# Two-layer hybrid trunk on one core: VectorE and ScalarE in the program's own order, and a weight tile's residual emitted with its load

## The chip, the cores and the metric

The kernel runs on one core of one Trainium2 chip. The metric is the device time of one execution in microseconds (us). A core has a tensor engine (TensorE, "PE" in the profile, its weight loads "PEld"), VectorE ("DVE"), ScalarE ("ACT"), GpSimd ("POOL") and SyncE ("SP"), which issues the transfers. The engines run side by side, each through its own instructions in the order in which they were emitted to it, and wait for one another by semaphores.

## The reference

256 tokens of width 2048 go through two layers. Each layer has a token mixer (layer 0: forgetting attention with 16 heads of 128; layer 1: grouped-query attention with 32 heads of 64 in a window of 128, with sinks and partly rotated positions) and a gated ConvFFN of inner width 5632. Cut to what matters:

```python
c_act = silu(c)
for i in range(2):
    mod = c_act @ ada_w[i] + ada_b[i]            # 2048 -> 6 x 2048
    sh1, sc1, g1, sh2, sc2, g2 = split(mod, 6)
    h = x * (1 + sc1) + sh1
    y = fox_attention(h) if i == 0 else swa_attention(h)
    x = layer_norm(alpha * x + (1 + g1) * y)
    h = x * (1 + sc2) + sh2
    y = conv_ffn(h)     # u = conv3(h @ w_up) + b; (silu(u[:5632]) * u[5632:]) @ w_down
    x = layer_norm(alpha * x + (1 + g2) * y)
# fox_attention: q, k, v, f = split(h @ w_in); C = cumsum(log_sigmoid(f + b))
#   softmax(q k^T / sqrt(128) + C_t - C_s, causal) @ v, then @ w_o
```

All data are float32.

## The kernel before, in words

**Products in three parts.** Each float32 operand of a large product is split into a high part and a residual. For a weight tile the high part `wh` is a cast on ScalarE (L254), and the residual `wl` = `w` − `wh` a subtraction on VectorE (L265). TensorE (L75, `mm`) then adds three products: high with high, high with residual, residual with high. The same split is made of activations by `split`: cast on ScalarE (L84), subtraction on VectorE (L85).

**Weight tiles.** `stream` loads weights through SyncE in tiles of 128x1024 values (two of the kernel's rows of tiles of 512 columns) into a pool of six 1 MB buffers, which the adaLN weights (`wa`) share. `wh` and `wl` have four buffers each. For each tile `stream` emits the load and the cast at once and appends a function `go` to the list `work`. `settle(2)` runs the oldest entries of `work` until no more than two tiles are outstanding. Before it runs one, `rest(f, *work)` emits the residuals of that tile and of the next ones, up to three tiles. `go` then runs the deferred work that is due (`run_post`), the products of the tile (`use`), one entry of `feeds`, and `tick`.

**What `tick` adds.** It hands out side work at a rate per weight tile: an adaLN column (L364, on VectorE, 128x2048), gate rows, and pieces of attention heads. A head of layer 0 is: scores `S`; two passes on VectorE that mask and find the maximum (L609, 128x128 and 128x256, with a readout `nm`); two exponentials with sums on ScalarE (L613); the reciprocal of the sums on VectorE (L621); two scalings on ScalarE (L623); transposes on TensorE (`T`, L640) and their copy (`pT`, L642); the product with the values, split into `oT`. Layer 1's heads come in pairs in a similar way (L609, L613, L961 to L972), with queries turned and split (`qT`, `qL`).

**Evacuations.** `evac_qk` adds the two halves of a projection on VectorE (`sum`, L756), and splits the sum: `qh` on ScalarE (L759 or L84), `ql` on VectorE (L760 or L85). The FFN's evacuation has a scaled copy `u` on ScalarE (L1006), two steps of the convolution on VectorE (L1007, L1009), the SiLU on ScalarE (L1025) for the gate half, the product (L1030) and the split into `gT` (L84, L85) for the other half.

**Between sub-layers.** `residual` (L537 multiply, L539 add, L544 to L549 statistics) evacuates the output projection by blocks of 512 columns, for token halves t = 0 and t = 1; then rows are normalised, modulated and split (`hH`). At the end of the program the last LayerNorm is written as a loop over t and four blocks, each with two operations on VectorE (L1095, L1096) and its transfer out.

**What sets the order.** The kernel is written for a framework that takes the program's order as a start and then lets a scheduler of its own order the instructions of each engine by when it expects them to be ready. Single instructions are held in place by `pin` (L78 to L81). Of the residuals (`residual_`) only those are held that are emitted while `behind[0] > 0`. The line that could take whole engines out of the scheduler's hands stands at the top, with an empty list, so that it does nothing.

Of the kernel before, what the change touches and what calls it, by code (L numbers as in the profile page):

```python
# [40 lines left out]
@with_exitstack  # L41
def hybrid_trunk(ctx: ExitStack, tc: tile.TileContext, a: dict, out: bass.AP):
    nc = tc.nc
    if []:
        ctx.enter_context(tc.manual_schedule(engines={getattr(mybir.EngineType, e) for e in []}))
    f32 = lambda t: t.bitcast(F32)

    cst = ctx.enter_context(tc.tile_pool(name="cst", bufs=1))
# [7 lines left out]
    def wtile(name="w"):  # L56
        return wp.tile([P, UK, WB], F32, tag="w", name=name)
# [19 lines left out]
    def pin(ins, on=True):  # L77

        if on:
            tc.keep_in_program_order(ins)  # L80
# [103 lines left out]
    feeds, post, work = [], [], []  # L184
# [11 lines left out]
    def settle(left=0):  # L196
        while work and (ahead[0] > left or not left):
            f = work.pop(0)
            rest(f, *work)
            f()  # L200

    def rest(*items):

        n = 0
        for f in items:
            if f in lone:
                n = max(n, 2)
            if f in residuals:
                residuals[f]()
                n += 1  # L210
            elif f in weights:
                n += 1
            if n > 2 - (items[0] not in weights):
                return
# [7 lines left out]
    def run_post():  # L222
        for g in list(post):
            if next(g, post) is post:
                post.remove(g)
# [7 lines left out]
    def stream(wsrc, row0, col, ks, use, spare={}):  # L233

        ks, pend = list(ks), {}
        for kc in ks[::2]:
            g = row0 + kc
            src = wsrc[g // UK, col // WB]
            if kc in pend:
                w = pend[kc]  # L240
            elif g % UK == 0 and kc + 2 in ks:
                W = wtile()
                pin(nc.sync.dma_start(W, src), False)
                w, pend[kc + 2] = W[:, :2], W[:, 2:]
            else:
                if halves:
                    w = halves.pop()
                else:
                    W = wtile()
                    w = W[:, :2]  # L250
                    halves.append(W[:, 2:])
                pin(nc.sync.dma_start(w, src[:, g % UK:g % UK + 2]), False)
            h, l = spare.get(kc) or (hl.tile([P, 2, WB], F32R, tag=n, name=n) for n in ("wh", "wl"))
            pin(nc.scalar.copy(h, w), False)  # L254

            def go(kc=kc, h=h, l=l):
                ahead[0] -= 1
                run_post()
                use(kc, h, l)
                if feeds:  # L260
                    feeds.pop(0)()
                tick()

            def residual_(w=w, h=h, l=l, go=go):
                pin(nc.vector.tensor_tensor(l, w, f32(h), op=ALU.subtract), behind[0] > 0)  # L265
                behind[0] -= 1
                del residuals[go]

            ahead[0] += 1
            weights.add(go)  # L270
            residuals[go] = residual_
            work.append(go)
            settle(2)

    def x_mm(ps, kc, h, l, stat, last, first=0, ts=range(NT), js=range(2)):
# [37 lines left out]
    def x_stationary(wsrc, col, k0, nk, stat, end=0):  # L313

        ps = x_banks()
        use = x_mm_end(ps, stat, nk, end) if end else lambda kc, h, l: x_mm(ps, kc, h, l, stat, nk - 1)
        stream(wsrc, k0, col, list(range(nk)), use, spares(nk) if end == 8 else {})
        return ps

    def w_stationary(wsrc, col):  # L320

        ps = w_banks()
        stream(wsrc, 0, col, list(range(KC)), lambda kc, h, l: w_mm(ps, kc, h, l))
        return ps
# [24 lines left out]
    def tick():  # L349
        ada_tick()  # L350
        if not feeds:
            side_step()
            step()
# [300 lines left out]
    def out_proj(oT, full, w_o, l):  # L654
        def stat(kc, t):
            while kc not in full:
                step()
            return oT[kc][0][:, t * P:(t + 1) * P], oT[kc][1][:, t * P:(t + 1) * P]

        ps = {d: x_banks() for d in range(2)}  # L660

        def part(d, ks):
            use = x_mm_end(ps[d], stat, KC, 2) if d == D // WB - 1 else                 lambda kc, h, l_: x_mm(ps[d], kc, h, l_, stat, KC - 1)
            stream(w_o, 0, d * WB, ks, use)

        for i, ks in enumerate((range(0, 8), range(8, 12))):
            then(lambda i=i: ada.update(rate=(0.72, 0.43)[l]))
            for d in range(2):
                part(d, list(ks))
        then(lambda: (ada_need(l, 2), ada.update(rate=(0.72, 0.65)[l])))  # L670
        for d in range(D // WB):
            if d < 2:
                part(d, list(range(12, KC)))
            else:
                ps[d] = x_banks()
                part(d, list(range(KC)))
            then(lambda d=d: defer(residual(ps[d], d, gates[l, 2], True)), d == D // WB - 1)
        then(lambda: (flush(), ada.update(gate_free=True)), True)
# [462 lines left out]
```

## Time and profile before

| what | value |
|---|---|
| median of 3 runs | 2195.59 us (2195.2 to 2195.61) |
| the profiled execution | 2194.81 us |
| its span | 2193.0 us |
| mean granted TensorE clock | 0.993 |
| busy TensorE / weight loads | 2138.1 us (97%) / 1948.5 us (89%) |
| busy VectorE / ScalarE | 1764.0 us (80%) / 1161.5 us (53%) |
| weight tiles split | 724 (`wh` 761.4 us on ScalarE, `wl` 879.4 us on VectorE) |
| adaLN columns | 192 (449.4 us on VectorE) |
| read from HBM | 594.18 MB, 272 GB/s over the span |

The span is the time from the first to the last instruction of the profiled execution; its own time is 1.8 us longer. Busy times are summed per engine over the whole span, so they average over stages which differ: the stages of layer 0's heads, the two FFNs, layer 1's heads and the transitions. In a group's line stand the line of the kernel, the engine, the operation, what is written and read (partitions x elements), the count, then busy us and mean ns of one, then the idle time of the engine just before and what ended it.

### The profile page before, as it was taken

What the parts mean: (1) busy time and instruction counts of PE and PEld (TensorE: products, weight loads), DVE (VectorE), ACT (ScalarE), POOL (GpSimd) and SP (SyncE); (2) the same over time, 40 slices, a digit from 0 to 9 for tenths busy, and PEclk for the clock granted to TensorE, in tenths of its full rate; (3) what the DMA queues carried; (4) which work ended last, traced back from release to release, by engine and by line L of the source; (5) the groups of instructions that cost most, each with busy time, mean ns of one, the idle gap of its engine ahead of it and who ended that gap; (6) DMA issues with size and microseconds to landing.
All of it is one profiled execution on the core that took longest, in us unless ns stands there. A gap on an engine that the chain in (4) does not pass through costs nothing.

```text
span 2193.0 us, 36167 instructions
## 1 busy us (share of the span) xinstructions
PE 2138.1 (97%) x14694; PEld 1948.5 (89%) x14694; DVE 1764.0 (80%) x2412; ACT 1161.5 (53%) x1771; POOL 11.5 (1%) x34
## 2 busy tenths in 40 slices
PE   6999999899999999999999999999999999999997
PEld 6999887689999888999987877789999988999986
DVE  7988899989989888898998876679787655666765
ACT  4546566355575433555554577555556533555541
POOL 1000000000000000000000000000000000000000
PEclk9999999999999999999999999999999999999999
DMA  9998999958878898887998653458776555555552
GB/s 385 421 373 307 359 340 338 346 205 343 325 281 324 325 364 341 321 316 284 329 349 308 238 189 130 154 175 305 272 268 248 192 194 193 195 197 196 193 196 98
DMA packets 89657, 598.63 MB, mean 273 GB/s; under 512 B 10017, under 2 KB 12353, under 8 KB 21137
## 3 DMA queue, kind: packets, MB, share of 16 engines
q1 hardware_dynamic: 89312, 595.87, 73.5%
q8 instruction: 115, 1.88, 0.3%
q0 software_dynamic: 176, 0.44, 0.1%
q14 instruction: 54, 0.43, 0.1%
HBM read 594.18 MB, written 2.10 MB: 272 GB/s over the span
## 4 chain that ended last, share of the span: by engine, by line
PE 85%; DVE 9%; ACT 3%; issue 2%; DMA 2%; SPq 0%; POOL 0%; DVEq 0%; ACTq 0%; POOLq 0%
PE ws L75 46%; PE xs L75 35%; DVE wa L364 3%; DVE wl L265 3%; DMA w<-in_fox_w_in_dram 2%; ACT wh L254 1%; PE o L75 1%; PE T L640 1%; PE S L75 1%; PE sm L446 0%; DVE x L581 0%; ACT pr L613 0%; DVE x L582 0%; DVE x L539 0%; DVE stats L544 0%
## 5 line engine op out<-in xcount | busy, mean ns | idle before, releaser
L254 ACT CAST wh<-w 128x1024 fp32r<-128x1024 f32 x724 | 761.4, 1053 | 804.4 <-PE xs L75 372.1
L265 DVE TENSOR_TENSOR wl<-w,wh 128x1024 fp32r<-128x1024 f32 x724 | 879.4, 1221 | 349.3 <-ACT wh L254 346.0
L75 PE MATMUL ws<-hH,wh 128*128 128x256 f32 x6656 | 1144.6, 276 | 8.6 <-ACT hH L473 7.5
L75 PEld LDWEIGHTS ws<-hH,wh 128*128 128x128 f32 x6656 | 1007.7, 188 | 13.5 <-ACT hH L473 7.9
L75 PE MATMUL ws<-hH,wl 128*128 128x256 f32 x3328 | 914.8, 276 | 4.3 <-DVE wl L265 4.3
L75 PEld LDWEIGHTS ws<-hH,wl 128*128 128x128 f32 x3328 | 625.0, 188 | 5.7 <-DVE wl L265 5.5
L364 DVE CUSTOM_DVE_ANT_0 wa<-wa,cb,acol 128x2048 f32<-128x2048 f32 x192 | 449.4, 2343 | 0.2 <-DVE cb L134 0.2
L75 PE MATMUL xs<-wh,gT 128*128 128x512 f32 x1376 | 424.6, 389 | 0.0
L75 PEld LDWEIGHTS xs<-wh,gT 128*128 128x128 f32 x1376 | 258.3, 188 | 53.6
L75 PE MATMUL xs<-wl,gT 128*128 128x512 f32 x688 | 267.7, 389 | 0.0
L75 PE MATMUL xs<-wh,hH 128*128 128x512 f32 x704 | 237.2, 403 | 2.8 <-ACT wh L254 2.8
L75 PEld LDWEIGHTS xs<-wh,hH 128*128 128x128 f32 x704 | 132.6, 190 | 32.8 <-ACT wh L254 3.4
L75 PEld LDWEIGHTS xs<-wl,gT 128*128 128x128 f32 x688 | 129.2, 188 | 26.7
L75 PE MATMUL xs<-wl,hH 128*128 128x512 f32 x352 | 139.9, 398 | 2.8 <-DVE wl L265 2.8
L75 PE MATMUL xs<-wh,oT 128*128 128x512 f32 x384 | 128.7, 405 | 0.0
L1006 ACT ACTIVATE u<-ws,ccol 128x256 f32<-128x256 f32 x176 | 96.8, 562 | 58.6 <-PE ws L75 46.0
L1007 DVE SCALAR_TENSOR_TENSOR u<-ws,ccol,u 128x255 f32<-128x255 f32 x176 | 82.4, 477 | 12.2 <-ACT u L1006 12.2
L75 PEld LDWEIGHTS xs<-wh,oT 128*128 128x128 f32 x384 | 74.1, 194 | 16.8 <-ACT oT L84 0.6
L1009 DVE SCALAR_TENSOR_TENSOR u<-ws,ccol,u 128x254 f32<-128x254 f32 x176 | 83.2, 477 | 2.2
L75 PE MATMUL xs<-wl,oT 128*128 128x512 f32 x192 | 77.4, 404 | 6.8 <-DVE wl L265 6.8
L75 PEld LDWEIGHTS xs<-wl,hH 128*128 128x128 f32 x352 | 66.7, 190 | 16.6 <-DVE wl L265 3.5
L613 ACT ACTIVATE pr<-pr,nm 128x128 f32<-128x128 f32 x96 | 43.2, 452 | 25.5 <-DVE nm L609 25.4
(195 smaller groups left out, 1103.3 us busy)
## 6 DMA issues: line engine op xcount, KB each, us to landing
wa<-in_ada_w_dram SPq DMA_DIRECT2D x192, 1024.0 KB, 7.1
w<-in_ffn_w_up_dram SPq DMA_DIRECT2D x176, 1024.0 KB, 5.7
w<-in_ffn_w_down_dram SPq DMA_DIRECT2D x88, 1024.0 KB, 5.0
w<-in_fox_w_in_dram SPq DMA_DIRECT2D x60, 512.0 KB, 8.6
w<-in_swa_w_in_dram SPq DMA_DIRECT2D x20, 1024.0 KB, 6.3
w<-in_fox_w_in_dram SPq DMA_DIRECT2D x18, 1024.0 KB, 7.3
w<-in_fox_w_o_dram SPq DMA_DIRECT2D x16, 1024.0 KB, 7.4
w<-in_swa_w_o_dram SPq DMA_DIRECT2D x16, 1024.0 KB, 4.7
```

The lines of the kernel that those rows point to most:

```text
L75: return nc.tensor.matmul(o, lhsT, rhs, start=start, stop=stop, **kw)
L254: pin(nc.scalar.copy(h, w), False)
L265: pin(nc.vector.tensor_tensor(l, w, f32(h), op=ALU.subtract), behind[0] > 0)
L364: return nc.vector.tensor_tensor_reduce(w, w, cb, 1.0, acol[:, l, v * KC + k:v * KC + k + 1], ALU.mult, ALU.add, cv[:, k:k + 1])
L613: nc.scalar.activation(pr[:, b:e], pr[:, b:e], AF.Exp, bias=nm[:, r:r + 1], scale=-1.0, accum_out=ss[:, r:r + 1])
L640: nc.tensor.transpose(tps[:, b * P:(b + 1) * P], pr[:, b * P:(b + 1) * P], ident)
L1006: nc.scalar.activation(u, pf, AF.Identity, bias=cw(CW, f), scale=cw(2, f))
L1007: nc.vector.scalar_tensor_tensor(u[:, 1:], pf[:, :S - 1], cw(1, f), u[:, 1:], op0=ALU.mult, op1=ALU.add)
L1009: nc.vector.scalar_tensor_tensor(u[:, 2:], pf[:, :S - 2], cw(0, f), u[:, 2:], op0=ALU.mult, op1=ALU.add)
```

## The change: two lines

The line at the top now names VectorE and ScalarE and is no longer conditional, so all of their instructions stay in the order in which the program emits them. TensorE's, GpSimd's and SyncE's stay in the scheduler's hands. And `stream` calls `rest(*work)` when it has appended a tile, before `settle(2)`: with nothing or one tile ahead, the new tile's residual is emitted at once. Lines 46 to about 270 move up by one, so that L265 before is L264 after and L254 is L253; from `x_mm` on the numbers are equal.

```diff
@@ hybrid_trunk
     nc = tc.nc
-    if []:
-        ctx.enter_context(tc.manual_schedule(engines={getattr(mybir.EngineType, e) for e in []}))
+    ctx.enter_context(tc.manual_schedule(engines={mybir.EngineType.DVE, mybir.EngineType.Activation}))
     f32 = lambda t: t.bitcast(F32)
...
@@ stream
             weights.add(go)
             residuals[go] = residual_
             work.append(go)
+            rest(*work)
             settle(2)
```

What this does to the order is shown at three places. The first is on VectorE, at a head of layer 0. Names: `wa` and `cv` an adaLN column, `pr` and `nm` a head's masked scores and maxima, `ss` the sums, `sum` and `ql` an evacuated projection and its residual. Before:

```order
L364 ISA wa,cv<-wa,cb,acol 128x2048
L364 ISA cv 128x1
L609 ISA pr,nm<-S,mask 128x128
L609 ISA nm 128x1
L609 ISA pr,nm<-S,mask 128x256
L609 ISA nm 128x1
L265 TENSOR_TENSOR wl<-w,wh 128x1024
L621 RECIPROCAL ss<-ss 128x2
L760 SCALAR_TENSOR_TENSOR ql<-sum,qh 128x512
```

After, at the same head:

```order
L364 ISA wa,cv<-wa,cb,acol 128x2048
L364 ISA cv 128x1
L609 ISA pr,nm<-S,mask 128x128
L609 ISA nm 128x1
L609 ISA pr,nm<-S,mask 128x256
L609 ISA nm 128x1
L621 RECIPROCAL ss<-ss 128x2
L264 TENSOR_TENSOR wl<-w,wh 128x1024
L756 TENSOR_TENSOR sum<-ws,gpart 128x512
L760 SCALAR_TENSOR_TENSOR ql<-sum,qh 128x512
```

The weight residual has moved from in front of the reciprocal to behind it, and `ql` stands directly behind its `sum`. On ScalarE, at the same place, before (`A` is a head's decay operand, `qh` a projection's high part):

```order
L613 ACTIVATE pr,ss<-pr,nm 128x128
L613 ACTIVATE pr,ss<-pr,nm 128x256
L773 ACTIVATE A<-A_150,sel 128x256
L623 ACTIVATE pr<-pr,ss 128x128
L623 ACTIVATE pr<-pr,ss 128x256
L773 ACTIVATE A<-A_150,sel 128x256
L254 CAST wh<-w 128x1024
```

After:

```order
L253 CAST wh<-w 128x1024
L759 ACTIVATE qh<-sum 128x512
L613 ACTIVATE pr,ss<-pr,nm 128x128
L613 ACTIVATE pr,ss<-pr,nm 128x256
L623 ACTIVATE pr<-pr,ss 128x128
L623 ACTIVATE pr<-pr,ss 128x256
L253 CAST wh<-w 128x1024
L642 COPY pT<-T 128x384
```

The scalings follow the exponentials with nothing between them, and the cast whose residual stands behind VectorE's reciprocal comes right behind the scalings. The third place is the end of the program on VectorE, from the last block's `residual` on. Before:

```order
L1095 SCALAR_TENSOR_TENSOR x<-x,mv,ln 128x512 x2
L1096 SCALAR_TENSOR_TENSOR x<-x,rs,ln 128x512 x2
L537 TENSOR_TENSOR t<-xs,gate 128x512
L539 TENSOR_TENSOR x<-x,t 128x512
L543 SCALAR_TENSOR_TENSOR rs<-mv,rs 128x1
L544 BN_STATS stats<-x 128x6
L547 BN_AGGR mv<-stats 128x2
L549 TENSOR_SCALAR mv<-mv 128x1
L1095 SCALAR_TENSOR_TENSOR x<-x,mv,ln 128x512 x2
L1096 SCALAR_TENSOR_TENSOR x<-x,rs,ln 128x512 x2
```

After:

```order
L537 TENSOR_TENSOR t<-xs,gate 128x512
L539 TENSOR_TENSOR x<-x,t 128x512
L543 SCALAR_TENSOR_TENSOR rs<-mv,rs 128x1
L544 BN_STATS stats<-x 128x6
L547 BN_AGGR mv<-stats 128x2
L549 TENSOR_SCALAR mv<-mv 128x1
L1095 SCALAR_TENSOR_TENSOR x<-x,mv,ln 128x512
L1096 SCALAR_TENSOR_TENSOR x<-x,rs,ln 128x512
L1095 SCALAR_TENSOR_TENSOR x<-x,mv,ln 128x512
L1096 SCALAR_TENSOR_TENSOR x<-x,rs,ln 128x512
```

The first half's eight final operations, which stood in front of the second half's last `residual`, now stand behind it, and they alternate where they stood in pairs. In all, 1248 rows of VectorE's order, 772 of ScalarE's, some 735 of TensorE's, 8 of SyncE's and 2 of GpSimd's differ. With `rest(*work)` alone, only two or three residuals in the opening move.

## The prediction

> **What bounds the kernel now.** I read the busy times first, then the chain of waits, then busy time by stage, and then, in the stages without room, who waits for whom. First the page's span and busy times, and the head of the chain that ended last:
>
> ```profile
> span 2193.0 us, 36167 instructions
> PE 2138.1 (97%) x14694; PEld 1948.5 (89%) x14694; DVE 1764.0 (80%) x2412; ACT 1161.5 (53%) x1771; POOL 11.5 (1%) x34
> PE 85%; DVE 9%; ACT 3%; issue 2%; DMA 2%; SPq 0%; POOL 0%; DVEq 0%; ACTq 0%; POOLq 0%
> ```
>
> TensorE is the bound on average: 97% busy, and 85% of the chain runs through it. VectorE has a fifth of the span free and ScalarE nearly half. On that average, waits on those two should cost nothing. But VectorE holds 9% of the chain, so somewhere it sets the pace. The windows say where (us of the stretch, busy PE, weight loads, DVE, ACT, POOL, granted clock, DMA share, GB/s):
>
> ```profile
> 200.00:445.00 245.00, 229.46 (x1345) 198.12 (x1344) 226.04 (x309) 133.81 (x262) 0.00 (x0) 0.97 0.91 344
> 445.00:515.00 70.00, 66.65 (x509) 61.90 (x509) 63.46 (x106) 39.24 (x54) 1.12 (x2) 1.00 0.59 214
> 515.00:735.00 220.00, 220.00 (x1914) 218.89 (x1913) 199.59 (x258) 129.68 (x198) 0.00 (x0) 1.00 0.86 320
> 1285.00:1400.00 115.00, 115.00 (x685) 87.68 (x685) 72.94 (x232) 85.26 (x220) 0.00 (x0) 0.99 0.37 128
> ```
>
> Row one is the stage of layer 0's attention heads with its output projection: VectorE is busy 226.04 of 245 us, as much as TensorE, and only 19.0 us are free. Row two is the first LN transition (6.5 us of VectorE free), row three the first FFN's up-projection (20.4 free, TensorE full), row four layer 1's heads (42.1 free, ScalarE the busier of the two). Waits from the start to 515 us (engine, line, who is waited for: total us, times, longest):
>
> ```profile
> PE xs L75 <- DVE wl L265: 9.6, 4, 4.2
> DVE t L537 <- PE xs L75: 7.0, 4, 3.2
> PE ws L75 <- DVE wl L265: 4.3, 6, 1.9
> PE ws L75 <- DVE hH L475: 0.8, 1, 0.8
> ```
>
> TensorE now waits 9.6 + 4.3 = 13.9 us for residuals there. That is what a better order could win.
>
> **The change, part by part.** The added `rest(*work)` moves one residual in front of one ada column in the opening, and beyond the opening the order is that of the pinned engines. The rest is the pinning. Nothing is added or taken away: the same instructions stand in a queue that can't be passed. So the question at every place is what VectorE stands still for that it now fills.
>
> **A, head stage.** Four heads come in a cluster, one per weight tile. Before, a residual or an ada column stands between the second score pass (L609) and the reciprocal (L621). Now the reciprocal follows L609 directly, and the next residual follows the reciprocal, while its high part on ScalarE stands behind both scalings (L623), which need the reciprocal. Rows of one head, VectorE and then ScalarE (start, length, operation):
>
> ```profile
> 215.76 0.42 DVE L609 CUSTOM_DVE_ANT_1 pr<-S,mask 128x256 f32<-128x256 f32 x1
> 218.38 0.15 DVE L621 RECIPROCAL ss<-ss 128x2 f32<-128x2 f32 x1
> 216.68 0.19 ACT L613 ACTIVATION_READ_ACCUMULATOR pr<-pr,nm 128x1 f32 x1
> 214.14 1.04 ACT L254 CAST wh<-w 128x1024 fp32r<-128x1024 f32 x1
> 212.96 0.79 ACT L623 ACTIVATE pr<-pr,ss 128x128 f32<-128x128 f32 x2
> 207.20 0.64 ACT L759 ACTIVATE qh<-sum 128x512 fp32r<-128x512 f32 x1 [1.19 <-DVE sum L756]
> ```
>
> L609 ends at 215.76 + 0.42 = 216.18, the sum of the exponentials is there at 216.68 + 0.19 = 216.87: the reciprocal now stands 0.69 us. The residual then stands 0.79 + 1.04 = 1.83 us for two scalings and a cast. Likewise `ql` (L760) now follows its `sum` (L756) directly and waits 0.64 us for the cast between them. The counts, from VectorE's groups in this window:
>
> ```profile
> L756 DVE TENSOR_TENSOR sum<-ws,part 128x512 f32<-128x512 f32 x8 | 5.3, 683 | 0.0
> L756 DVE TENSOR_TENSOR sum<-ws,gpart 128x512 f32<-128x512 f32 x4 | 2.6, 680 | 0.0
> L621 DVE RECIPROCAL ss<-ss 128x2 f32<-128x2 f32 x16 | 2.5, 158 | 0.2
> ```
>
> 16 × 0.69 = 11.0, 16 × 1.83 = 29.3, 12 × 0.64 = 7.7: 48.0 us of new standing. VectorE's free 19.0 us can take some, and what is over lengthens the stage, since 226.0 + 48.0 = 274 exceeds 245: **+29.0**. Ends: 0 if TensorE's two or three ready tiles and the free time absorb it all, +48.0 if the free time stays where it is (the waits for TensorE at L537 above are part of it). I take the middle account because most free time is waits for TensorE or for a cast, which shrink when VectorE is late. The 13.9 us are not booked as a gain: TensorE waited for residuals because VectorE was full, and it gets fuller.
>
> **B, first LN transition.** Each of six normalised rows gets its cast on ScalarE and its residual directly behind, so VectorE stands 0.62 per row, and the weight residual behind it 1.05 − 0.69 = 0.36 for its own cast (ScalarE's groups in this window, then a group of VectorE's over the run):
>
> ```profile
> L84 ACT CAST hH<-t 128x512 fp32r<-128x512 f32 x6 | 3.6, 616 | 2.3 <-DVE t L464 2.3
> L254 ACT CAST wh<-w 128x1024 fp32r<-128x1024 f32 x22 | 23.0, 1051 | 20.8 <-PE ws L75 9.8 <-PE xs L75 8.6 <-issue 1.5
> L85 DVE TENSOR_TENSOR hH<-t,hH 128x512 fp32r<-128x512 f32 x25 | 17.1, 687 | 3.4 <-ACT hH L84 3.1
> ```
>
> 6 × 0.98 = 5.9 against 6.5 free, half of it the fixed wait for the projection's end: **+3** (0 to 5.9).
>
> **C, the FFNs.** The gated product's residual now stands directly behind the product and waits for ScalarE's cast (ScalarE's group in the third window):
>
> ```profile
> L84 ACT CAST gT<-u 128x256 fp32r<-128x256 f32 x20 | 8.1, 403 | 3.8 <-DVE u L1030 3.7
> ```
>
> At most 8.1 us on 199.6, which makes 207.7 of 220: hidden under TensorE's full 220, with 12 us of cover left: **0** (0 to 8.1). Were VectorE 12 us later from the stages ahead, the tiles ready for TensorE would run out, and this would show.
>
> **G, layer 1's heads.** Here the residual now follows two score passes and waits for the second exponential (0.50 + 0.19) and the cast (1.05), 1.74 us, and `oT` and `qL` wait for their casts (ScalarE's groups in the fourth window):
>
> ```profile
> L613 ACT ACTIVATE pr<-pr,nm 128x256 f32<-128x256 f32 x25 | 12.6, 502 | 0.0
> L613 ACT ACTIVATION_READ_ACCUMULATOR pr<-pr,nm 128x1 f32 x50 | 9.4, 189 | 0.0
> L84 ACT CAST oT<-o 128x256 fp32r<-128x256 f32 x11 | 4.0, 365 | 0.0
> L84 ACT CAST qT<-qp 128x512 fp32r<-128x512 f32 x5 | 2.9, 579 | 0.0
> ```
>
> 72.9 + 25 × 1.74 + 4.0 + 2.9 = 123.3 against 115: between 0 (some of it overlaps) and +8.3; I take the middle, **+4**.
>
> **D, the tail.** The final normalisation of the first token half (eight operations L1095 and L1096) runs now while TensorE finishes the second half. In program order it stands behind the second half's statistics, and each L1096 right behind the L1095 it depends on. VectorE at the end:
>
> ```profile
> 2172.80 1.40 DVE L1095 SCALAR_TENSOR_TENSOR x<-x,mv,ln 128x512 f32<-128x512 f32 x2
> ...
> 2181.34 0.69 DVE L537 TENSOR_TENSOR t<-xs,gate 128x512 f32<-128x512 f32 x1 [3.17 <-PE xs L75]
> 2182.07 0.69 DVE L539 TENSOR_TENSOR x<-x,t 128x512 f32<-128x512 f32 x1
> ...
> 2183.89 1.41 DVE L1095 SCALAR_TENSOR_TENSOR x<-x,mv,ln 128x512 f32<-128x512 f32 x2
> ...
> 2187.87 1.41 DVE L1096 SCALAR_TENSOR_TENSOR x<-x,rs,ln 128x512 f32<-128x512 f32 x2
> ```
>
> Eight operations, independent in pairs, take 2183.89 to 2189.28, 5.39 us. A dependent pair has a pitch of 2182.07 − 2181.34 = 0.73. So 16 × 0.73 − 5.39 = **+6.3**; +5.4 if dependent neighbours overlap as pairs do. Nothing covers this: TensorE has ended. [...] The rows with 0.73 and 0.67 (5.39 / 8) differ a little, so I keep the measured pitch.
>
> **E, opening.** One residual moves ahead of one ada column, one activation residual one column later: **0** (−0.8, the wait on `hH` above, to +2.3, one column).
>
> **F, the clock.** After TensorE's longest wait, its rows read:
>
> ```profile
> 437.11 0.79 PE L75 MATMUL xs<-wl,oT 128*128 128x512 f32 x1 [4.22 <-DVE wl L265]
> 437.70 1.05 PE L75 MATMUL xs<-wh,oT 128*128 128x512 f32 x2
> 438.56 0.63 PE L75 MATMUL xs<-wl,oT 128*128 128x512 f32 x1
> ...
> 442.07 0.63 PE L75 MATMUL xs<-wh,oT 128*128 128x512 f32 x2
> 442.54 0.40 PE L75 MATMUL xs<-wl,oT 128*128 128x512 f32 x1
> ```
>
> Two products take 0.86 us at first and 0.47 five microseconds later: a wait of 4.22 cost at most 5.0 × 0.45 = 2.2 us more in slow products. New standing comes in pieces of 0.7 to 1.8 us, shorter than that, and VectorE is the slower one then: **0**, with +8.8 (one such slow start for each of the four clusters) as the other end. [...]
>
> **Sum.** 29.0 + 3 + 0 + 4 + 6.3 + 0 + 0 = 42.3 on the profiled execution's 2194.81 gives 2237.1; the median of the runs (2195.59) is 0.8 higher, so **2238**.
>
> **The rivals.**
> *Faster (chance 0.08).* In program order no residual stands behind an ada column that nobody needs. If ScalarE's answers fit into the free 19 us, the 13.9 us of waits for residuals go and only the tail is paid: 2195.6 − 13.9 + 6.3 = 2188. It decides at 19 us: of 48 us of standing, 60% must overlap with present waits. The waits of TensorE speak for it, 226 of 245 against.
> *Hidden (0.10).* TensorE's 97% covers all, and only the tail shows: 2195.6 + 6.3 = 2202. The third window speaks for it, the first against. [...]
> *Heavier (0.18).* Free time stays unused (A 48.0), and B, C, G and the clock take their upper ends: 48.0 + 5.9 + 8.1 + 8.3 + 6.3 + 8.8 = 85.4, 2281; halfway to it 2260 to 2270. For it speaks that four heads come in a row; against it that two to three tiles lie ready.
> *No effect of the pins (0.04).* If TensorE's own order decides, the sum of the changes is within 0.2% of now, 2191 to 2200.
>
> **Numbers.** The main case, 2215 to 2260, has 0.60. The range to 2200 and 2288 takes in the hidden case and the upper ends and leaves out faster and no effect. A change of under 0.2% (4.4 us) is about what a measurement of this kernel can't tell from none: faster 0.08, same 0.05, slower 0.87.
>
> **What would show it.** Right: the head stage grows by some 30 us, waits of L621 for L613 and of the residual for its cast rise there to tens of us, TensorE's waits for residuals exceed 13.9, the FFN windows keep TensorE full, and sixteen final operations follow the last L549. Wrong: the head stage is no longer than 245 us, with VectorE's standing in place of its present free time; or the FFN stages, which I cost at nothing, lose TensorE's full rows.

## The result, and the profile after

The changed kernel took 2317.2 us (median of 4 runs, 2315.34 to 2318.71) against 2195.46 (2195.2 to 2195.61) beside it: 1.0554 times as long, with a 95% interval of 1.0536 to 1.0573. That is 122 us slower; the prediction was 2238, 42 us slower, with 2288 as its upper end. The direction came out as argued, and so did the standing for ScalarE's answers; what would cover it, and where else it would fall, did not. The page of the changed kernel, its span, busy times and the shares of the chain that ended last:

```profile
span 2315.3 us, 36181 instructions
PE 2196.0 (95%) x14694; PEld 1967.3 (85%) x14694; DVE 1799.3 (78%) x2412; ACT 1143.7 (49%) x1771; POOL 11.1 (0%) x34
PE 66%; DVE 18%; ACT 9%; issue 4%; DMA 2%; SPq 0%; POOL 0%; ACTq 0%; DVEq 0%; POOLq 0%
```

The averages hardly move: each engine's share is two to four points lower. The chain moves a lot: VectorE's and ScalarE's part of it went from 12% to 27%. To see where, both kernels were cut at the same places of the work, at the start of the same weight residual (number 58, 112, 128 and so on of the 724 on VectorE, counted from 0). Before, in windows (us, then busy PE, weight loads, DVE, ACT, POOL, granted clock, DMA share, GB/s), for layer 0's heads, the end of its output projection, and the first transition:

```profile
201.00:396.00 195.00, 186.97 (x1178) 164.75 (x1179) 182.64 (x260) 118.96 (x247) 0.00 (x0) 0.99 0.92 347
396.00:448.00 52.00, 45.19 (x179) 35.70 (x178) 43.70 (x48) 15.43 (x15) 0.00 (x0) 0.90 0.86 319
448.00:524.00 76.00, 72.65 (x574) 68.43 (x573) 71.23 (x117) 42.28 (x59) 1.12 (x2) 1.00 0.65 244
```

After, the same three, and behind them the second transition and layer 1's attention:

```profile
202.00:447.00 245.00, 209.44 (x1173) 174.23 (x1173) 183.27 (x257) 116.83 (x243) 0.00 (x0) 0.93 0.74 274
447.00:494.00 47.00, 40.81 (x167) 31.53 (x166) 46.47 (x50) 15.25 (x15) 0.00 (x0) 0.96 0.93 360
494.00:583.00 89.00, 78.81 (x566) 71.80 (x565) 74.94 (x121) 40.57 (x58) 1.12 (x2) 0.96 0.58 219
1265.00:1329.00 64.00, 57.40 (x244) 43.06 (x243) 42.88 (x61) 41.13 (x81) 0.00 (x0) 0.97 0.51 182
1329.00:1520.00 191.00, 178.71 (x970) 131.01 (x970) 126.82 (x352) 117.98 (x284) 0.00 (x0) 0.99 0.43 149
```

In the heads VectorE does the same work (182.64 and 183.27 us), but its free time grows from 12.4 to 61.7 us, and the stretch by 50. Behind them the output projection is 5 us shorter than before, the one of these stretches where the new order wins. With the starts of the residuals to a tenth, the 122.3 us by which the span grew are:

| stretch (residuals) | before, us | grew by, us |
|---|---|---|
| opening (to 58) | 200.8 | +1.3 |
| layer 0's heads (58 to 112) | 195.1 | +50.3 |
| end of its output projection (112 to 128) | 52.5 | −5.7 |
| first transition (128 to 150) | 75.9 | +13.7 |
| FFN of layer 0 (150 to 394) | 674 | +8.1 |
| second transition and first projections (394 to 410) | 47 | +15.1 |
| layer 1's heads and output projection (410 to 456) | 177 | +15.2 |
| third transition (456 to 480) | 80 | +11.6 |
| FFN of layer 1, to TensorE's last product | 679 | +6.5 |
| behind TensorE's last product | 12.1 | +6.2 |

Some experiments move the residuals themselves, so that a residual's number marks another place of the work. There the end of TensorE's n-th matmul (counted from 0) is compared with the same one before; every kernel has 14694 of them, in nearly the same order. The difference is called the lag.

One head of layer 0 after the change, VectorE's rows and then ScalarE's (start, length, and in brackets the idle time before and what ended it):

```profile
315.45 0.42 DVE L609 CUSTOM_DVE_ANT_1 pr<-S,mask 128x256 f32<-128x256 f32 x1
316.59 0.17 DVE L621 RECIPROCAL ss<-ss 128x2 f32<-128x2 f32 x1 [0.71 <-ACT pr L613]
318.56 1.23 DVE L264 TENSOR_TENSOR wl<-w,wh 128x1024 fp32r<-128x1024 f32 x1 [1.80 <-ACT wh L253]
316.79 0.80 ACT L623 ACTIVATE pr<-pr,ss 128x128 f32<-128x128 f32 x2 [0.23 <-DVE ss L621]
317.50 1.03 ACT L253 CAST wh<-w 128x1024 fp32r<-128x1024 f32 x1
```

Predicted were 0.69 and 1.83; there are 0.71 and 1.80, in every head. The waits of VectorE over the stretch of the heads, after (total, times, longest):

```profile
DVE wl L264 <- ACT wh L253: 41.8, 23, 8.4
DVE ss L621 <- ACT pr L613: 11.3, 16, 0.7
DVE ql L760 <- ACT qh L759: 4.3, 6, 0.8
DVE ql L84 <- ACT qh L83: 4.2, 6, 0.7
```

### The profile page after: what moved, and what is told of

Same layout as the page of the kernel before. It is cut to its first block, busy times and chain, and to the rows that moved or that the text cites. A ratio compares the mean times of both kernels' runs of the same rounds, so it can differ in the third digit from the quotient of the medians.

```text
span 2315.3 us, 36181 instructions
## 1 busy us (share of the span) xinstructions
PE 2196.0 (95%) x14694; PEld 1967.3 (85%) x14694; DVE 1799.3 (78%) x2412; ACT 1143.7 (49%) x1771; POOL 11.1 (0%) x34
## 4 chain that ended last, share of the span: by engine, by line
PE 66%; DVE 18%; ACT 9%; issue 4%; DMA 2%; SPq 0%; POOL 0%; ACTq 0%; DVEq 0%; POOLq 0%
PE ws L74 39%; PE xs L74 27%; DVE wl L264 7%; DVE wa L364 5%; ACT wh L253 3%; ACT pr L613 2%; DMA wa<-in_ada_w_dram 1%; ACT dl L401 1%; ACT dh L401 1%; DVE x L581 1%; ACT pr L623 1%; ACT hH L83 0%; DVE t L464 0%; DVE u L1009 0%; DVE u L1007 0%
## 5 line engine op out<-in xcount | busy, mean ns | idle before, releaser
L74 PE MATMUL ws<-hH,wh 128*128 128x256 f32 x6656 | 1159.2, 278 | 19.2 <-ACT wh L253 7.2
L264 DVE TENSOR_TENSOR wl<-w,wh 128x1024 fp32r<-128x1024 f32 x724 | 875.6, 1222 | 363.1 <-ACT wh L253 359.7
L253 ACT CAST wh<-w 128x1024 fp32r<-128x1024 f32 x724 | 754.0, 1051 | 604.4 <-PE xs L74 286.6
L74 PE MATMUL ws<-hH,wl 128*128 128x256 f32 x3328 | 919.6, 279 | 15.3 <-DVE wl L264 14.7
L74 PEld LDWEIGHTS ws<-hH,wl 128*128 128x128 f32 x3328 | 628.5, 190 | 21.3 <-DVE wl L264 21.1
L74 PE MATMUL xs<-wh,hH 128*128 128x512 f32 x704 | 244.5, 413 | 14.9 <-ACT wh L253 10.5
L74 PE MATMUL xs<-wl,hH 128*128 128x512 f32 x352 | 146.4, 416 | 8.4 <-DVE wl L264 8.1
L83 ACT CAST gT<-u 128x256 fp32r<-128x256 f32 x88 | 35.8, 407 | 237.4 <-DVE u L1030 237.4
L74 PEld LDWEIGHTS xs<-wl,hH 128*128 128x128 f32 x352 | 68.9, 196 | 29.7 <-DVE wl L264 15.6
```

Source lines behind the costliest of these rows:

```text
L74: return nc.tensor.matmul(o, lhsT, rhs, start=start, stop=stop, **kw)
L83: nc.scalar.copy(h, src)
```

## The experiments

The theory is that time goes where VectorE and ScalarE stand for each other's answers with nothing else to do. The rivals are that the added call does it, that one engine's order alone does it, or that residuals coming too late for TensorE do it. Each kernel was timed beside the kernel before (2194.9 to 2195.6).

**The call alone** (`only_rest`): before, with the one added line.

```diff
             work.append(go)
+            rest(*work)
             settle(2)
```

> Before, with the added call of rest alone; no engine is pinned. If the time comes from the pinned order, nothing changes: 2195 within 4 us. If emitting a residual with its load were what costs (it displaces work on VectorE), the time would go most of the way to 2317.

It took 2193.96 us, ratio 0.9994 (0.9985 to 1.0004): no change. The call is not the cause.

**The pinning alone** (`manual_no_rest`): the changed kernel without that line.

> The changed kernel without the added call of rest: only the pinning. With VectorE alone pinned and no such call, the first residual came 13 us late and some 6 us of that were left behind the opening, so the call should be worth about 6 us under the pinning although it was worth nothing without it: 2323, between 2319 and 2327. If it does nothing here either: 2317 within 4.

2321.39 us, ratio 1.0575 (1.0557 to 1.0593), 4 us above the changed kernel with intervals that overlap. In its trace the first residual starts 10.5 us later, and at residual 58 it is 3.0 us behind the changed kernel; so the call is worth some 3 us under the pinning, half of what was expected, and nothing without it.

**One engine at a time** (`only_dve`, `only_act`): before, with the list at the top holding one name.

```diff
-    if []:
-        ctx.enter_context(tc.manual_schedule(engines={getattr(mybir.EngineType, e) for e in []}))
+    ctx.enter_context(tc.manual_schedule(engines={mybir.EngineType.DVE}))
```

> Before, with VectorE alone in program order; ScalarE is ordered by the scheduler, which puts the weight casts two tiles ahead of the heads' exponentials. If VectorE loses time by standing for answers of ScalarE, the 1.8 us per head for the cast go and the 0.7 for the reciprocal, the 0.64 of ql, the 0.74 per normalised row and the 6.2 of the tail stay: 11 + 8 + 13 + 6 on 2195, about 2233, between 2215 and 2255. If VectorE's order were the whole of it, 2317. If it were ScalarE's order alone, 2195 plus the tail's 6, 2201.

> Before, with ScalarE alone in program order. The casts stand behind the scalings as in the changed kernel, so a residual still can't start before them, but VectorE may put other work (an ada column, a sum) in front of it. By the standing theory part of 16 x 1.8 us in layer 0's heads and of 28 x 1.6 in layer 1's is filled and the tail keeps its old order: about 2235, between 2205 and 2280. If ScalarE's late casts alone were the cause, some 2311 (2317 without the tail's 6).

VectorE alone took 2248.77 us (1.0246, 1.023 to 1.0261), ScalarE alone 2240.37 (1.0203, 1.0188 to 1.0218). Neither is the whole: 54 and 45 us of 122; the two pins together cost 22 more than that sum. VectorE's waits in the heads differ as the order says; with VectorE alone pinned:

```profile
DVE ss L621 <- ACT pr L613: 15.0, 16, 1.5
DVE ql L760 <- ACT qh L759: 9.0, 6, 5.2
```

and with ScalarE alone pinned:

```profile
DVE wl L265 <- ACT wh L254: 30.8, 21, 2.1
DVE ss L621 <- ACT pr L613: 7.2, 11, 0.8
```

A scheduled ScalarE puts its casts early, and the 1.8 us per head are gone; a scheduled VectorE still can't have a residual before its cast. The heads grew by 15.3 us in the first and 30.7 in the second: nearly the 19 (16 × 0.71 + 12 × 0.64) and the 29 (16 × 1.8) of standing that each keeps.

**The residual one tile later** (`resid_later`).

```diff
-            if n > 2 - (items[0] not in weights):
+            if n > 1 - (items[0] not in weights):
```

> The changed kernel with one number altered in rest: a residual is emitted one tile later, so VectorE reaches it when ScalarE's cast has long run; nothing else moves. By the standing theory 16 x 1.8 = 29 us go in layer 0's heads, 18 x 0.26 = 5 in the transitions and some 15 to 20 in layer 1's heads: about 2265, between 2245 and 2285. By the rival that TensorE needs the residuals early (a shorter lead starves it), it is no faster than 2317 and TensorE's waits for residuals rise.

2273.02 us, ratio 1.0354 (1.0338 to 1.0369): 44 us less than the changed kernel. VectorE's second statistics (L547), behind the output projection, start at 457.8 us before, at 503.7 in the changed kernel and at 473.6 here: 15.8 us behind before instead of 45.9. That is 30.1 us less, close to the 29 of 16 × 1.8. VectorE's waits in the heads:

```profile
DVE ss L621 <- ACT pr L613: 13.3, 16, 1.4
DVE wl L264 <- ACT wh L253: 6.9, 2, 6.0
DVE ql L760 <- ACT qh L759: 6.1, 6, 2.5
```

What the cast behind the scalings cost is gone, what the reciprocal and `ql` cost is still there. The rival has a small part too: through the first transition (matmuls 2669 to 3784) the lag grows by 19.6 us, from 15.8 to 35.4, where the changed kernel's grows by 16.4, and TensorE's waits for weight residuals there are 12.1 us in 8 pieces against 4.9 in 4. So the shorter lead costs some 3 us there.

**Heads taken apart** (`late_heads`): `resid_later`, and the reciprocal and scalings one step later, and both sums in front of the first split.

```diff
-        pr = probs(sps)
...
+        pr = exps(sps, nm, ss)
+        yield
+        nc.vector.reciprocal(ss, ss)
...
         yield
```

> resid_later (2273) with layer 0's heads taken apart: reciprocal and scalings one step of the head later than the score passes, and both sums of a projection in front of the first cast's residual. By the standing theory 16 x 0.71 + 12 x 0.64 = 19 us go: 2254, between 2250 and 2262, and VectorE's waits at the reciprocal and at ql are near zero. By the rival that the shorter lead of the residuals sets the pace in this stage now, it stays within 4 us of 2273.

2263.23 us, ratio 1.0311 (1.0296 to 1.0327): 10 us less where 19 were expected, 1 us outside the range. The waits at the reciprocal (13.3) are gone from VectorE's list, those of `ql` fell from 10.3 to 6.4, and the second statistics come 6.9 us behind before instead of 15.8. Part of the rest turned into a wait that was 1.0 in `resid_later`, for the cast of `oT`, and one wait of 6.0 of a weight residual stays as in `resid_later`:

```profile
DVE wl L264 <- ACT wh L253: 8.2, 4, 6.0
DVE oT L84 <- ACT oT L83: 6.6, 6, 2.5
```

**Normalised pairs later** (`late_feeds`): `resid_later`, and the residual of a normalised pair emitted one feed later.

```diff
-        split(hH[:, k:k + 2, :], hL[:, k:k + 2, :], tmp.rearrange("p (j s) -> p j s", j=2))
...
+        nc.scalar.copy(h, src)
+        sub = lambda: nc.vector.tensor_tensor(l, src, f32(h), op=ALU.subtract)
...
+            late.append(sub)
```

> resid_later (2273) with the residual of a normalised pair emitted one feed later, so that a weight residual stands between it and ScalarE's cast. By the standing theory up to 18 x 0.74 = 13 us of standing go in the three transitions, of which some 10 are on the path: 2263, between 2258 and 2270. If the transitions are slow because rows are normalised, turned and modulated one after another (TensorE's turn in between), it stays within 4 us of 2273.

2265.03 us, ratio 1.0319 (1.0304 to 1.0335): 8 us less. VectorE's waits in the first transition, in `resid_later` and then here:

```profile
DVE t L464 <- PE sm L446: 5.4, 3, 2.9
DVE hH L84 <- ACT hH L83: 4.5, 6, 0.7
```

```profile
DVE t L464 <- PE sm L446: 6.2, 5, 2.9
```

The wait for the cast is gone. That for TensorE's turn of rows that VectorE has just normalised stays; it was not in the prediction.

**The tail** (`tail_early`): the changed kernel with the final LayerNorm of a token half emitted inside `residual`, two blocks at a time, right behind its statistics.

```diff
                     moments[t] = (mv[:, 0:1], rs[:, 0:1], rs[:, 1:2])
+                    if end:
+                        finish(t)
```

> The changed kernel with the last LayerNorm of the first token half written in front of the second half's last evacuation, and its operations in pairs, as the scheduler had them; nothing else. If the tail is worth the 6.2 us by which the time behind TensorE's last product grew (12.1 to 18.3): 2311, between 2309 and 2313, with 12 us from TensorE's last product to the end. If the longer tail only fills time that the transfer out takes anyway: 2317.

2307.87 us, ratio 1.0514 (1.0498 to 1.0529): 9 us less, 1 us outside the range on the faster side. The part behind TensorE's last product is read from the trace:

```profile
2293.39 0.39 PE L74 MATMUL xs<-wh,gT 128*128 128x512 f32 x1
```

To the span's end at 2305.4 it is 12.1 us, as in the kernel before (12.1), against 18.3 in the changed one: 6.3 us are the tail. The other 3.6 us came in before that, most of them between residuals 480 and 560, where the span grew by 3.7 us here and in `manual_no_rest` and by 6.5 in the changed kernel. The edit doesn't reach there, and why they differ is left open.

**All four together** (`late_all`).

> The changed kernel with all four edits together: residuals one tile later, heads taken apart, the normalised pairs' residuals one feed later, the last LayerNorm early. If the gains of the single runs add (44 + 10 + 8 + 6 or 9 on 2317): 2248, between 2244 and 2253. What would then be left, some 50 us over before, is not standing for a cast that an edit of the order took away; if the gains come out of the same free time they do not add, and it is over 2253.

2250.01 us, ratio 1.0253 (1.0239 to 1.0267). The single gains nearly add (71 of them, 67 measured). What is left, 55 us, lies by the lag mostly in the three transitions (15.4, 12.5 and 10.1); the heads and the output projection have 6.3 of it and the FFN of layer 0 has 5.0. VectorE's largest wait in the first two is that for TensorE's turned rows (L464: 6.0 and 7.4 us). No run takes that wait away, so what holds the transitions stays open.

**VectorE alone, with the same edits** (`dve_all`): `only_dve` with the call, heads taken apart, pairs later and tail early, but the full lead.

> VectorE alone in program order (only_dve: 2249), with the added call of rest and with heads taken apart, normalised pairs' residuals one feed later and the last LayerNorm early; residuals keep their full lead and ScalarE stays with the scheduler. If only_dve's 54 us are 6 in the opening, some 16 in layer 0's heads, 29 in the transitions and 6 in the tail, these edits take 5 + 12 + 12 + 6: 2214, between 2204 and 2228. If VectorE's free time has to be filled by a scheduler, not by hand, it stays over 2235.

2209.8 us, ratio 1.0069 (1.0055 to 1.0082): 39 us less than `only_dve`. An order by hand for one engine comes close to the scheduler's. In the heads it is 0.6 us slower than before, in the output projection 5.7 faster; the loss is in the opening (2.5), the first and third transitions (8.5 and 5.3) and the FFN of layer 0 (2.4).

**Only the residuals held** (`pin_resid`): before, with `behind[0] > 0` replaced by `True` at the residual's `pin`.

> Before, with no engine pinned but every weight residual held in program order against the ada columns (the condition on behind taken off). Reciprocals, sums and the tail stay with the scheduler. If TensorE's 13.9 us of waits for residuals come from ada columns put in front of due residuals, some go: 2188, between 2183 and 2194. If they come from VectorE being full in that stage, nothing changes: 2195 within 4.

2211.29 us, ratio 1.0078 (1.0064 to 1.0092): 0.8% slower, and the expectation was wrong. The first residual starts 12.4 us later, held behind ada columns, of which 2.9 are left at residual 58; the heads lose 5.2 and the first and third transition 5.1 and 4.6. TensorE's longest wait for a residual is now in the first transition (460 to 560 us):

```profile
PE ws L75 <- DVE wl L265: 8.2, 2, 7.6
```

**Held in one stage** (`held_stage`): no engine pinned; VectorE's instructions are held from layer 0's first full projection to the end of its output projection, through a wrapper that calls `keep_in_program_order` while a flag is set; with the added call, and heads taken apart as above.

> No engine pinned. VectorE's instructions are held in program order from layer 0's first full projection to the end of its output projection alone, with the heads taken apart as in late_heads and the added call of rest; transitions, FFNs, layer 1 and the tail stay with the scheduler. dve_all came from 2.5 us behind before at this stage's start to 2.6 ahead at its end: by that a gain of 5 us, 2190, between 2186 and 2194. If the scheduler needs VectorE free in this stage to keep ScalarE and TensorE in step, or if the gain is given back at the next transition, 2195 within 4.

2191.7 us, ratio 0.9984 (0.9975 to 0.9993): 0.16% faster than the kernel before. The same two stretches as above (heads, output projection):

```profile
201.00:397.00 196.00, 186.01 (x1166) 163.16 (x1165) 180.72 (x257) 117.19 (x244) 0.00 (x0) 0.99 0.91 346
397.00:444.00 47.00, 42.97 (x178) 33.65 (x177) 46.32 (x54) 15.68 (x15) 0.00 (x0) 0.96 0.93 351
```

The heads are 0.6 us longer than before; the gain, 4.5 us in the span, is in the output projection (5.7), and it is not given back. There, before, the scheduler has VectorE stand 3.2 us at a `residual` (L537) for TensorE with two weight residuals behind it, and TensorE stands 4.2 us for a weight residual a little later, with the slow products quoted in the prediction behind that. Held, VectorE's only wait for ScalarE in this stretch is 0.3 us, TensorE's longest for a weight residual from 201 to 445 us is 2.4, and the granted clock is 0.96 against 0.90. No run has the call and the heads taken apart without the hold; but `only_dve`, which has neither, is shorter by the same 5.7 us in the output projection.

## Why the prediction was right in direction and wrong in size

The forecast added 42.3 us and 122.3 came. Of the 80 us between, 15.6 lie in stage A, 10.7 in the first transition, 26.7 in the two later ones, which had no term, 14.6 in the FFNs, which were put at nothing, 11.2 in layer 1's heads, and 1.2 in the opening and the tail together. Both kinds of sign that the prediction named showed: TensorE's waits for residuals up to the first FFN rose to 20.8 us from 13.9, and the FFNs lost TensorE's full rows.

**A, heads and output projection: +29.0 predicted, +44.6 measured (+50.3 in the heads, −5.7 behind them).** The 48.0 us of standing were right: 11.3 at the reciprocal, 28.8 (16 × 1.80) for the cast behind the scalings and 8.5 at `ql` make 48.6. The failed step is the cover: "226.0 + 48.0 = 274 exceeds 245", which lets the stage's 19 free us take some of the standing. That free time lay elsewhere. From 200 to 445 us of before, VectorE stood for casts:

```profile
DVE wl L265 <- ACT wh L254: 12.3, 9, 4.0
```

And 6.5 of the 19 us lie in the output projection (VectorE busy 42.47 of 49 us from 396 to 445), 7.2 between the first two rows of heads (37.81 of 45 from 245 to 290). Heads come four in a row, where VectorE had next to none. The first such row, before:

```profile
200.00:245.00 45.00, 43.91 (x312) 40.32 (x311) 44.75 (x66) 30.70 (x58) 0.00 (x0) 1.00 0.91 348
```

0.25 of 45 us free. The old free time didn't shrink either: beside the 28.8 us, the waits for casts in the heads after hold another 13.0, of which 8.4 at 283 us, where the cast stands behind a gate row's scalings (see C). So the upper end, +48.0, was the answer for the heads, and `resid_later` and `only_dve` give back or keep the pieces nearly one to one.

**B, transitions: +3 predicted, +13.7 measured; the second and third were given nothing and cost 15.1 and 11.6.** Per normalised row the rows after read:

```profile
513.49 0.54 DVE L464 TENSOR_SCALAR t<-sm,G,B 128x256 f32<-128x256 f32 x1 [0.65 <-PE sm L446]
514.77 0.69 DVE L84 TENSOR_TENSOR hH<-t,hH 128x512 fp32r<-128x512 f32 x1 [0.74 <-ACT hH L83]
515.72 1.22 DVE L264 TENSOR_TENSOR wl<-w,wh 128x1024 fp32r<-128x1024 f32 x1 [0.26 <-ACT wh L253]
```

The predicted 0.62 + 0.36 is 0.74 + 0.26 here, right again; missing is the wait for TensorE's turn (0.65 here, three times, 1.9 in all), and again the cover was counted where it couldn't be used: VectorE's free time in the stretch grew from 4.4 to 13.8 us, and its busy time, with one weight residual more, from 71.5 to 75.8. The two later transitions have the same rows and were passed over; in the third VectorE's free time grew from 13.1 to 21.1 us. In the second a gate row comes on top (what it is stands under C). Its 32 scalings ran in the FFN in front before (1121 to 1135 us), and in program order they stand among the transition's casts (1289 to 1306 us; ScalarE's rows, then VectorE's):

```profile
1290.07 1.27 ACT L401 ACTIVATE dl<-ident,gl 128x128 fp32r<-128x128 f32 x4
1291.24 1.03 ACT L253 CAST wh<-w 128x1024 fp32r<-128x1024 f32 x1
1292.31 1.23 DVE L264 TENSOR_TENSOR wl<-w,wh 128x1024 fp32r<-128x1024 f32 x1 [2.60 <-ACT wh L253]
```

Four residuals stand 9.1 us there (2.60, 2.06, 2.07 and 2.33). With ScalarE alone pinned the gate row lies in this transition too, which grows by 9.8 us; with VectorE alone pinned it lies in front, and the transition grows by 4.6.

**C, FFNs: 0 predicted, 8.1 and 6.5 measured.** The split of `gT` alone is covered, as said: from residual 200 to 394, with TensorE's products as dense as before, the time even fell by 1.3. But from residual 150 to 200 TensorE was busy for 140.3 of 144.2 us, where it had been for all of 134.7. The miss is an instruction that the prediction did not look at. A gate row spreads its column over a diagonal with eight scalings per tile on ScalarE (L401), and in program order they stand ahead of the weight cast (ScalarE's rows, then VectorE's):

```profile
678.06 1.27 ACT L401 ACTIVATE dh<-ident,gh 128x128 fp32r<-128x128 f32 x4
679.24 1.26 ACT L401 ACTIVATE dl<-ident,gl 128x128 fp32r<-128x128 f32 x4
680.41 1.03 ACT L253 CAST wh<-w 128x1024 fp32r<-128x1024 f32 x1
681.48 1.23 DVE L264 TENSOR_TENSOR wl<-w,wh 128x1024 fp32r<-128x1024 f32 x1 [2.06 <-ACT wh L253]
```

Three residuals stand 8.2 us (3.25, 2.06 and 2.86) at this gate row, where two stood 4.9 before, and four stand 11.5 us at that of layer 1's FFN (6.5 in five pieces before). The lag grows mainly at these two places: from 62.3 to 66.7 us at the first (605 to 640 us of before) and from 110.0 to 116.1 at the second (1680 to 1711). From 661 to 1066 us of before it grows by 0.3, and from 1711 us to TensorE's last product not at all. With either engine pinned alone it doesn't grow at these two places. What the gate rows cost is read from the rows and these places; no run took them out.

**G, layer 1's heads: +4 predicted, +15.2 measured.** The standing of 1.74 per residual was near, 1.6 in the rows. VectorE's waits from 1329 to 1420 us:

```profile
DVE wl L264 <- ACT wh L253: 25.7, 16, 1.6
```

Two steps failed. The sum books all 25 waits as new, but VectorE stood in the same way before; in the prediction's own window, 1285 to 1400 us:

```profile
DVE wl L265 <- ACT wh L254: 37.3, 28, 2.6
```

And it takes the window's 42.1 free us, most of which are this very standing, as cover, and halves what is left over. From residual 410 to 428 the waits for casts grew from 11.0 us (9) to the 25.7 (16) above, 14.7 of the 17.9 us by which that part grew. From matmul 8243 to 9234 (heads and output projection) the lag grows by 20.0 us in the changed kernel, and by 2.7 with the residual one tile later, so the standing for the cast is nearly all of it.

**D, the tail: +6.3 predicted, +6.2 measured.** Sixteen operations from 2299.99 to 2311.73, 0.73 each:

```profile
2299.99 0.74 DVE L1095 SCALAR_TENSOR_TENSOR x<-x,mv,ln 128x512 f32<-128x512 f32 x1
2300.77 0.75 DVE L1096 SCALAR_TENSOR_TENSOR x<-x,rs,ln 128x512 f32<-128x512 f32 x1
2301.44 0.75 DVE L1095 SCALAR_TENSOR_TENSOR x<-x,mv,ln 128x512 f32<-128x512 f32 x1
...
2310.98 0.75 DVE L1096 SCALAR_TENSOR_TENSOR x<-x,rs,ln 128x512 f32<-128x512 f32 x1
```

In these rows an operation starts 0.78 us after the one it needs (2299.99 to 2300.77; one of the eight 0.85), and one that needs nothing from its neighbour 0.67 after it (2300.77 to 2301.44). The 0.73 that the prediction took for every step is what the two come to on average.

**E, opening: 0 predicted, +1.3.** Right.

**F, the clock: 0 predicted.** TensorE's granted clock in the heads fell from 0.99 to 0.93. The reason given for the 0, that standing of 0.7 to 1.8 us is too short for that, failed. In a row of heads (the clock is the third number from the end):

```profile
324.00:331.00 7.00, 5.91 (x15) 4.08 (x16) 4.46 (x6) 3.47 (x6) 0.00 (x0) 0.64 0.75 277
```

TensorE's waits at its start are 1.53, 0.50 and 0.53 us. What the slower clock cost beside the standing can't be separated here, since VectorE set the pace in those rows; the growth of its free time (49.3 us) nearly accounts for the stretch without it. From 222 to 242 us, with a wait of 3.39 in it, the clock was 0.83; in the row above it was 0.64, with no wait over 1.55 from 290 us on; and from 290 to 300 us it was 1.00, with one of 1.54. So the length of a wait alone doesn't tell here what the clock does, and no run shows a price.

Of the rivals, "heavier" named the right mechanism (free time stays unused), and even its upper end of 2281 was short by the transitions, the gate rows and layer 1.

## What to carry to other kernels

Free time of an engine in a stage is no cover for new standing unless it lies where the standing is: cut the stage down to the cluster, and count standing in full where the engine is busy without a break (48.6 us of standing here, and the heads grew by 50.3). When two engines that answer each other are both put in program order, expect every split of one value over both (cast here, subtraction there) to become a wait: the sum goes over all such pairs in the program, not over the three that one looks at, and whatever else stands in front of the cast (here a gate row) counts too. Subtract the standing that the kernel has already. Emitting the second half one step later took most of the wait away here (6.9 us in the heads instead of 41.8), at the price of a shorter lead (some 3 us in the first transition). Where a scheduler has misplaced a few instructions, try to hold that stretch alone; it won 0.16% here.

## What the runs showed that was not expected

The two pins are more than the sum of each: 54 and 45 us alone, 122 together. The rows fit the reading that a scheduled engine fills in around a fixed one (with VectorE alone pinned, ScalarE's casts come early and the 1.8 us per head are gone), but how the 22 us split over the stages was not worked out. And holding one kind of instruction is worse than holding none: with the residuals alone held against the ada columns, the kernel lost 16 us, where 7 were expected to be won.
